# First mixer of a two-layer decode and prompt step: cached attention by halves of the heads, in four phases per group

## The chip, the cores and the metric

The program runs on one core of a Trainium2 chip. The core has five engines that work at once: TensorE (PE, matrix products; PEld are its weight loads), VectorE (DVE), ScalarE (ACT), GpSimd (POOL) and SyncE (SP, which here only issues transfers). Its 16 DMA engines bring data from HBM into the on-chip memory SBUF. The metric is the device time of the program in microseconds. The kernel before took 2915.26 us, the median of 3 runs (2914.95 to 2918.68).

## The reference, cut to what matters

The program does one step of a two-layer model for a prompt of 272 positions (16 of them meta tokens) and for 8 sequences that each bring 4 new tokens and have 2048 cached ones, in pages of 128. The change is in layer 0, in the attention of the 8 sequences over their cached pages. Each of the 8 heads has two score maps (m) over the same values, and the second is subtracted with a learned factor:

```python
def diff_attn_core(q, qpos, segs, lam):
    slopes = alibi_slopes(N_DH)
    qf = q.astype(jnp.float32) * (DK ** -0.5)
    scores = []
    for k, v, kpos in segs:
        s = jnp.einsum('bqhmd,bshmd->bhmqs', qf, k.astype(jnp.float32))
        dist = (qpos[:, None] - kpos[None, :]).astype(jnp.float32)
        s = s - slopes[None, :, None, None, None] * jnp.abs(dist)
        scores.append(jnp.where(dist >= 0, s, -jnp.inf))
    p = jax.nn.softmax(jnp.concatenate(scores, axis=-1), axis=-1)
    ...
    return out[:, :, :, 0] - lam * out[:, :, :, 1]

        k_past = cache_k[e, page_table].reshape(B, past_len, N_DH, 2, DK)
        v_past = cache_v[e, page_table].reshape(B, past_len, N_DH, DV)
        qpos = past_len + jnp.arange(T, dtype=jnp.int32)
        o = diff_attn_core(q, qpos, [(k_past, v_past, jnp.arange(past_len, dtype=jnp.int32)), (k, v, qpos)], lam)
```

Beside it in the same mixer stand the input projection (query, key, value, two convolution halves), the prompt's own attention, a causal depthwise convolution of width 31 with a layer norm, and the output projection. Everything is float32.

## The kernel before

All activations lie with their 2048 features over 16 tiles of 128 partitions and the 304 positions (272 of the prompt, 8 times 4 of the sequences) along the free dimension. A weight matrix is streamed as panels of 256 columns; a panel of the input projection is four *weight units* of 512 KB. ScalarE rounds a unit to a high part (`whi`, line 157), VectorE computes the rest (`wlo`, line 167), and TensorE makes three products for each of its eight tiles (lines 238 to 240), 24 in all.

Units and cache pages come through one ring of nine slots of 512 KB (`K.run`). SP issues all these transfers in program order, each as soon as its slots are free: line 118 a weight unit, line 1111 a key page, line 1194 a value page. A page's number is read from the page table in SBUF by SP itself just ahead of its transfer (`page`, lines 1099 to 1101), and the transfer's address is computed from it.

The decode attention works by two groups of four sequences. A *key unit* is two pages of keys of one sequence (two slots): eight products of 256 columns (line 1123), four heads beside each other in the four 32-column strips of TensorE's array. After the four sequences of a chunk, ScalarE copies the scores into `S` and VectorE takes the maxima (lines 1129, 1130). When all 16 pages are through, `k_new` (scores of the new tokens, maximum, four exponentials, line 1149), nine `transposes` (lines 1176 to 1185) and `k_norm` follow in one block. A *value unit* is one page (one slot): four products of 256 columns (line 1200). `v_copy` scales the sums of a sequence, `v_extract` picks out the diagonal pieces. New keys and values come from the projection of the same step (`k_done`, `v_done`).

The order is written out by `build`: `decode_jobs` lists the decode work, and `mix(i, W)` merges `SLOTS[i]` slots of it evenly with a stretch W of the weight panels. `tick` emits the pieces of the prompt's attention (`p_q` to `p_ln2`) and of the convolution (`tap`, line 1336) in between, by estimated time. The seven stretches are called stages 0 to 6 below; before, stage 0 holds six panels of keys and values and 62 slots, stage 1 the other two panels with a first one of the convolution, stages 3 and 4 the convolution's panels, stage 5 no weights, stage 6 the output projection's first half. The output projection's second half (`o_half`) needs all heads and ends the mixer.

Of the kernel before, what the change touches and what calls it, by code (L numbers as in the profile page):

```python
# [17 lines left out]
P = 128  # L18
T = 304
# [631 lines left out]
SLOTS = ((62,), (58,), (2,), (54,), (28,), (28,), (24,))  # L651
# [16 lines left out]
def const_l0():  # L668
# [4 lines left out]
    for e in range(2):  # L673
        for n in range(4):
            for u in range(4):
                c[:, C_E + e * 16 + n * 4 + u] = (q == n) & (j == 2 * (n % 2) + e) & (t == u)
# [6 lines left out]
    for hf in range(2):  # L683
        sl = np.array([SLOPES[4 * hf + a] for a in j])
        for g in range(2):
            for k in range(32):
                ok = (k // 4 == 4 * g + b4) & (k % 4 <= t)
                c[:, C_NB + g * 64 + hf * 32 + k] = np.where(ok, sl * (k % 4 - t), -BIG)
        for ch in range(8):
            base = 32 * (ch % 4) + 2 * hf  # L690
            o = C_BL + ch // 4 * P
            c[base, o:o + P] = sl
            c[base + 1, o:o + P] = sl * (256 * (ch - 7) - t)
            c[base, C_BR + 256 * hf:C_BR + 256 * hf + 256] = np.arange(256) - 256
            c[base + 1, C_BR + 256 * hf:C_BR + 256 * hf + 256] = 1.0
# [8 lines left out]
class L0(Sched):  # L704
# [4 lines left out]
    def __init__(self, k):  # L709
        self.k, self.nc = k, k.nc  # L710
        super().__init__(3)
        self.first, self.main, self.tail = self.queues
        self.low, self.debt = [], 0.0
        self.last = {}
        self.low_at = []
        self.gate = False
        self.st, self.al, self.pvs_, self.late = {}, {}, {}, []
        self.rvp = {}
        self.new_ready, self.waiting, self.pvs = False, [], {}


    def build(self):
# [25 lines left out]
        mix(0, kv[:30])  # L748
        mix(1, kv[30:] + cc[:4])
# [67 lines left out]
    def pan(self, name):  # L817
        return self.k.pp.tile([P, 512], F32, name=name, tag="side", bufs=2)


    def enter(self):
# [18 lines left out]
        self.mx = ap.tile([P, 2, 9], F32, name="mx")  # L840
        self.sc = ap.tile([P, 8], F32, name="scol")
# [116 lines left out]
    def p_v(self, h, j, st):  # L958
# [15 lines left out]
        nc.scalar.copy(self.vn[:, hc], pv[:32, 384:512])  # L974
        st["v"] = (vh, vl)
        st["vl"] = low

    def p_vl(self, st):
        for o, a, b in st.pop("vl"):
# [54 lines left out]
    def p_at(self, st, part):  # L1034
# [3 lines left out]
        pa = self.pan("pat")  # L1038
        if part == 0:
# [45 lines left out]
    def make_q(self):  # L1085


        nc = self.nc
        for g in range(2):
            for m in range(2):  # L1090
                r = slice(64 * m, 64 * m + 64)
                src = self.q[r, :, NP_ + 16 * g:NP_ + 16 * g + 16].rearrange("p h (b t) -> p h b t", b=4)
                a = self.qb[r, g]
                dst = bass.AP(tensor=a.tensor, offset=a.offset + 4 * m, ap=[a.ap[0], [P, 8], [40, 4], [1, 4]])
                nc.vector.tensor_copy(dst, src)
                d = self.qd[r, g].rearrange("p h (b m t) -> p h b m t", b=4, m=2)[:, :, :, m]
# [6 lines left out]
    def k_unit(self, b, c):  # L1103
# [4 lines left out]
        def load(raw):  # L1108
            for u in range(2):
                v = self.page(b, 2 * c + u)  # L1110
                nc.sync.dma_start(raw[:, u * 1024:(u + 1) * 1024],
                                  k.ins["ck"][bass.ds(v, 1)].rearrange("o p n -> p (o n)"))

        def use(raw):
            if b4 == 0:
                self.psS = k.pp.tile([P, 512], F32, name="psS", tag="cache", bufs=1)
                base, o = 32 * (c % 4), c // 4 * P
                nc.tensor.matmul(self.psS, self.bl[base:base + 4, o:o + P], self.bl[base:base + 4, 2 * P:],
                                 start=True, stop=False, tile_position=(base, 0))
            rv = raw.rearrange("p (u h s) -> p u h s", u=2, h=8)  # L1120
            for hf in range(2):
                for j in range(4):
                    nc.tensor.matmul(self.psS[32 * j:32 * j + 32, hf * 256:hf * 256 + 256],  # L1123
                                     self.qb[:, g, 4 * hf + j, 32 * b4:32 * b4 + 32], rv[:, :, 4 * hf + j],
                                     start=False, stop=(b4 == 3 and hf == 1), tile_position=(0, 32 * j))
            if b4 == 3:
                S = self.S[:, :, c * 256:c * 256 + 256]
                ps = self.psS.rearrange("p (h s) -> p h s", h=2)
                nc.scalar.copy(S, ps)
                nc.vector.tensor_reduce(self.mx[:, :, c], S, axis=AX.X, op=ALU.max)  # L1130
        return Job(use, load, 2 * UNIT, False, 2)

    def k_new(self, g):
        nc = self.nc
        ps = self.pan("psN")
        for h in range(8):
            hf, j = divmod(h, 4)
            nc.tensor.matmul(ps[32 * j:32 * j + 32, hf * 32:hf * 32 + 32], self.qd[:, g, h], self.kn[:, h],
                             start=(hf == 0), stop=(hf == 1), tile_position=(0, 32 * j))
        S = self.S[:, :, 2048:]  # L1140
        nb = self.cst[:, C_NB + 64 * g:C_NB + 64 * g + 64].rearrange("p (h s) -> p h s", h=2)
        nc.vector.tensor_tensor(S, ps[:, :64].rearrange("p (h s) -> p h s", h=2), nb, op=ALU.add)
        nc.vector.tensor_reduce(self.mx[:, :, 8], S, axis=AX.X, op=ALU.max)
        nm = self.sc[:, 0:2]
        nc.vector.tensor_reduce(nm, self.mx, axis=AX.X, op=ALU.max, negate=True)
        for z, cols in enumerate((slice(0, 1024), slice(1024, 2080))):
            for hf in range(2):
                s = self.S[:, hf, cols]
                nc.scalar.activation(s, s, AF.Exp, bias=nm[:, hf:hf + 1],
                                     accum_out=self.sc[:, 2 + 2 * z + hf:3 + 2 * z + hf])  # L1150

    def k_norm(self, g):

        nc = self.nc
        rv = self.sc[:, 6:8]
        nc.vector.tensor_tensor(rv, self.sc[:, 2:4], self.sc[:, 4:6], op=ALU.add)
        nc.vector.reciprocal(rv, rv)
        nc.vector.tensor_scalar(rv, rv, self.ls, None, op0=ALU.mult)
        rm = self.ap.tile([P, 2, 4], F32, name="rm")
        nc.vector.tensor_tensor(rm, self.cst[:, C_B4:C_B4 + 4].unsqueeze(1).to_broadcast([P, 2, 4]),  # L1160
                                rv.unsqueeze(2).to_broadcast([P, 2, 4]), op=ALU.mult)
        ps = self.pan("psr")
        for hf in range(2):
            nc.tensor.matmul(ps[64 * hf:64 * hf + 64, :4], self.cst[:, C_SEL:C_SEL + 64], rm[:, hf], start=True, stop=True,
                             tile_position=(0, 64 * hf))
        self.rvp[g] = self.ap.tile([P, 4], F32, name="rvp", bufs=2)
        nc.scalar.copy(self.rvp[g], ps[:, :4])

    def transposes(self, part):
# [3 lines left out]
        if part < 8:  # L1173
            for i in range(4):
                hf, pg = i // 2, 2 * part + i % 2
                nc.tensor.transpose(tr[:, i * P:i * P + P], self.S[:, hf, pg * P:pg * P + P], k.ident)
            for hf, copy in ((0, nc.scalar.copy), (1, nc.vector.tensor_copy)):
                src = tr[:, 256 * hf:256 * hf + 256].rearrange("p (g j b m) -> p g b j m", g=2, j=4, b=4)
                dst = self.S[:, hf, 256 * part:256 * part + 256].rearrange("p (g b j m) -> p g b j m", g=2, b=4, j=4)
                copy(dst, src)  # L1180
        else:
            for hf in range(2):
                nc.tensor.transpose(tr[:32, hf * P:hf * P + P], self.S[:, hf, 2048:], k.ident)
                src = tr[:32, hf * P:hf * P + P].rearrange("p (j b m) -> p b j m", j=4, b=4)
                nc.scalar.copy(self.PN[:, hf].rearrange("p b (j m) -> p b j m", j=4), src)

    def v_unit(self, b, pg):
# [4 lines left out]
        def load(raw):  # L1192
            v = self.page(b, pg)
            nc.sync.dma_start(raw, k.ins["cv"][bass.ds(v, 1)].rearrange("o p n -> p (o n)"))

        def use(raw):
            if pg == 0:
                self.pv = k.pp.tile([P, 512], F32, name="pvp", tag="cache", bufs=1)
            for n in range(4):
                nc.tensor.matmul(self.pv[32 * n:32 * n + 32, :256], self.S[:, n // 2, pg * P + 32 * b4:pg * P + 32 * b4 + 32],  # L1200
                                 raw[:, n * 256:n * 256 + 256], start=(pg == 0), stop=(pg == 15 and not self.new_ready), tile_position=(0, 32 * n))
            if pg == 15 and self.new_ready:
                self.new_values(self.pv, b4, False)
            if pg == 15:
                self.v_copy(b)
        return Job(use, load, UNIT, False)

    def new_values(self, ps, b4, start):
        for n in range(4):
            self.nc.tensor.matmul(ps[32 * n:32 * n + 32, :256], self.PN[:, n // 2, b4],  # L1210
                                  self.vn[:, n * 256:n * 256 + 256], start=start, stop=True, tile_position=(0, 32 * n))

    def v_copy(self, b):
        self.pvs[b] = self.ap.tile([P, 256], F32, name="pvs", bufs=4)
# [939 lines left out]
```

## Time and profile before

| | |
|---|---|
| runs, median (lowest to highest) | 2915.26 us (2914.95 to 2918.68) |
| profiled execution, its own time | 2920.92 us |
| its span, first to last instruction | 2919.2 us |
| TensorE, VectorE, ScalarE busy | 96%, 62%, 44% of the span |
| moved by DMA | 607.42 MB, mean 208 GB/s |
| mean granted TensorE clock | 0.977 of full |

The span is that of the one profiled execution. In a group, "x128" counts instructions, the busy time is that of the group together (overlaps counted once), and "idle before" with an arrow names what ended the wait. The trace counts two instructions for each matrix product of plain float32, so 64 key units of eight products stand as x1024. TensorE's products overlap, so the mean duration of one is longer than its share of the busy time.

### The profile page before, as it was taken

How to read it: one execution, taken by the hardware profiler on the slowest of the kernel's cores; microseconds unless marked ns; L12 is line 12 of the kernel's file. 1: busy time of each engine (PE TensorE's matmuls, PEld its weight loads, DVE VectorE, ACT ScalarE, POOL GpSimd, SP SyncE). 2: the span in 40 equal slices, each digit the busy share in tenths (PEclk: the TensorE clock that was granted, in tenths of full speed). 3: DMA queues.
4: the chain of work that ended last, by engine and by line, in shares of the span. 5: the costliest groups of instructions: out<-in, count | busy, mean ns of one | idle time of the engine just before them, and what ended most of it. 6: DMA issues, size and time to landing. Idle time of an engine off the chain costs nothing.

```text
span 2919.2 us, 56571 instructions
## 1 busy us (share of the span) xinstructions
PE 2794.5 (96%) x22621; PEld 2649.8 (91%) x22621; DVE 1801.1 (62%) x3153; ACT 1273.3 (44%) x2257; POOL 181.3 (6%) x417
## 2 busy tenths in 40 slices
PE   8998898698999999999999999899999999999997
PEld 8776676388999999999999999899899999999997
DVE  6454489735776677677676688655754454554555
ACT  4344222334534544544445567444534333333343
POOL 1011100001000111111110012000000000000000
PEclk9999999799999999999999999999999999999999
DMA  6887989794445656656665668565355555545553
GB/s 232 304 294 286 335 304 347 282 345 149 152 149 185 203 187 203 217 185 199 216 196 182 209 228 305 177 201 164 127 170 162 172 161 169 166 157 178 160 161 103
DMA packets 169914, 607.42 MB, mean 208 GB/s; under 512 B 20225, under 2 KB 22690, under 8 KB 169394
## 3 DMA queue, kind: packets, MB, share of 16 engines
q1 hardware_dynamic: 147522, 522.58, 54.0%
q0 software_dynamic: 20688, 76.24, 7.3%
q10 hardware_dynamic: 1440, 4.98, 0.5%
q8 instruction: 177, 2.90, 0.4%
q14 instruction: 87, 0.71, 0.1%
HBM read 563.63 MB, written 40.10 MB: 207 GB/s over the span
## 4 chain that ended last, share of the span: by engine, by line
PE 73%; DVE 5%; issue 5%; DMA 2%; ACT 2%; POOL 1%; SPq 0%; DVEq 0%; POOLq 0%; ACTq 0%
PE pan L238 23%; PE pan L239 23%; PE pan L240 23%; DMA ring<-in_w_cc 1%; PE pvp L1200 1%; DVE wlo L167 1%; DMA scr<-scra 1%; DVE oc L1336 1%; DVE odd L1336 1%; PE stp L1785 0%; ACT whi L157 0%; PE yps L2013 0%; POOL scr L1900 0%; DMA ring<-in_cv 0%; PE skp L1793 0%
## 5 line engine op out<-in xcount | busy, mean ns | idle before, releaser
L167 DVE TENSOR_TENSOR wlo<-ring,whi 128x1024 fp32r<-128x1024 f32 (+1 forms) x738 | 884.1, 1201 | 677.7 <-ACT whi L157 674.2
L157 ACT CAST whi<-ring 128x1024 fp32r<-128x1024 f32 (+1 forms) x738 | 758.7, 1029 | 1121.4 <-PE pan L239 922.6
L238 PE MATMUL pan<-hh,whi 128*128 128x304 f32 (+1 forms) x3936 | 1204.7, 306 | 23.4 <-ACT hh L506 16.5
L240 PE MATMUL pan<-hh,wlo 128*128 128x304 f32 (+1 forms) x3936 | 1188.7, 302 | 11.7 <-DVE wlo L167 11.7
L239 PE MATMUL pan<-hl,whi 128*128 128x304 f32 (+1 forms) x3936 | 1188.0, 302 | 1.8 <-DVE hl L509 1.5
L238 PEld LDWEIGHTS pan<-hh,whi 128*128 128x128 f32 x3936 | 749.5, 190 | 56.9 <-issue 24.0
L240 PEld LDWEIGHTS pan<-hh,wlo 128*128 128x128 f32 x3936 | 749.3, 190 | 15.6 <-DVE wlo L167 15.6
L239 PEld LDWEIGHTS pan<-hl,whi 128*128 128x128 f32 x3936 | 749.6, 190 | 4.7 <-DVE hl L509 4.5
L238 PE MATMUL pan<-mh,whi 128*128 128x304 f32 (+1 forms) x1408 | 422.1, 300 | 0.0
L240 PE MATMUL pan<-mh,wlo 128*128 128x304 f32 (+1 forms) x1408 | 419.8, 298 | 0.0
L239 PE MATMUL pan<-ml,whi 128*128 128x304 f32 (+1 forms) x1408 | 419.7, 298 | 0.0
L238 PEld LDWEIGHTS pan<-mh,whi 128*128 128x128 f32 x1408 | 265.0, 188 | 1.0 <-issue 1.0
L240 PEld LDWEIGHTS pan<-mh,wlo 128*128 128x128 f32 x1408 | 265.1, 188 | 0.0
L239 PEld LDWEIGHTS pan<-ml,whi 128*128 128x128 f32 x1408 | 264.9, 188 | 0.0
L1200 PE MATMUL pvp<-ring,xs 128*32 128x256 f32 x1024 | 78.1, 432 | 12.6 <-DMA ring<-in_cv 7.4
L579 DVE TENSOR_TENSOR u<-g,u 128x304 f32<-128x304 f32 (+1 forms) x88 | 41.1, 467 | 69.1 <-ACT g L578 67.2
L393 DVE TENSOR_TENSOR sqa<-sqa,sqt 128x304 f32<-128x304 f32 (+1 forms) x78 | 36.6, 469 | 58.9 <-ACT sqt L389 57.8
L386 POOL MEMSET sqt<- 128x80 f32 x4 | 0.7, 165 | 1131.7 <-DVE sqa L393 1131.7
L577 DVE TENSOR_TENSOR u<-pan,rs 128x304 f32<-128x304 f32 (+1 forms) x88 | 40.8, 464 | 46.1 <-PE pan L240 46.1
L1200 PEld LDWEIGHTS pvp<-ring,xs 128*32 128x32 f32 x1024 | 29.8, 120 | 43.5 <-issue 13.8
L581 DVE TENSOR_TENSOR ml<-u,mh 128x304 fp32r<-128x304 f32 (+1 forms) x88 | 41.1, 467 | 44.5 <-ACT mh L580 44.5
L1123 PE MATMUL psS<-ring,qb 128*32 128x256 f32 x1024 | 67.0, 387 | 0.0
(371 smaller groups left out, 2885.2 us busy)
## 6 DMA issues: line engine op xcount, KB each, us to landing
ring<-in_w_gu SPq DMA_DIRECT2D x352, 512.0 KB, 3.6
ring<-in_ck SPq DMA_DIRECT2D x128, 512.0 KB, 5.7
ring<-in_cv SPq DMA_DIRECT2D x128, 512.0 KB, 6.0
ring<-in_w_dn SPq DMA_DIRECT2D x128, 512.0 KB, 3.7
ring<-in_w_qkv SPq DMA_DIRECT2D x48, 512.0 KB, 7.1
ring<-in_w_dn SPq DMA_DIRECT2D x64, 384.0 KB, 3.1
ring<-in_w_cc SPq DMA_DIRECT2D x32, 512.0 KB, 6.7
ring<-in_w_oe SPq DMA_DIRECT2D x32, 512.0 KB, 6.5
```

The lines of the kernel that those rows point to most:

```text
L157: nc.scalar.copy(j.hi[:, :n], j.raw[:, :n])
L167: nc.vector.tensor_tensor(j.lo[:, :n], j.raw[:, :n], j.hi[:, :n].bitcast(F32), op=ALU.subtract)
L238: mm(out, wh, xh, start=start, stop=False)
L239: mm(out, wh, xl, start=False, stop=False)
L240: mm(out, wl, xh, start=False, stop=stop)
L393: nc.vector.tensor_tensor(self.sq[:, c0:T], self.sq[:, c0:T], t[:, c0:T], op=ALU.add)
L577: nc.vector.tensor_tensor(u, pu, rs, op=ALU.mult)
L579: nc.vector.tensor_tensor(u, g, u, op=ALU.mult)
L581: nc.vector.tensor_tensor(self.ml[:, m, c0:], u, self.mh[:, m, c0:].bitcast(F32), op=ALU.subtract)
L1123: nc.tensor.matmul(self.psS[32 * j:32 * j + 32, hf * 256:hf * 256 + 256], self.qb[:, g, 4 * hf + j, 32 * b4:32 * b4 + 32], rv[:, :, 4 * hf ...
L1200: nc.tensor.matmul(self.pv[32 * n:32 * n + 32, :256], self.S[:, n // 2, pg * P + 32 * b4:pg * P + 32 * b4 + 32], raw[:, n * 256:n * 256 + ...
L1336: nc.vector.scalar_tensor_tensor(c, src, w, c, op0=ALU.mult, op1=ALU.add)
```

## The change

The head halves (heads 0 to 3, heads 4 to 7) are taken apart. The caches are laid out with the half as an outer index, a transfer brings half a page (128 partitions by 512 elements), and `half_page` reads the page number for each. A key unit is four half pages of one sequence (two slots), a value unit two half pages of consecutive pages (one slot). Each group has four phases: keys of half 0, keys of half 1, values of half 0, values of half 1; the softmax steps of a half stand between the units of the phase after it. Three query panels come ahead of the decode work instead of four, the fourth goes into stage 0 with all eight key and value panels, and `SLOTS` changes. `hold` has two subtractions of the prompt's attention emitted before their bank is taken again.

```diff
-SLOTS = ((62,), (58,), (2,), (54,), (28,), (28,), (24,))
+SLOTS = ((56,), (56,), (2,), (48,), (28,), (28,), (34,))
...
-        js, off = k.panels("w_qkv", 0, 4, ks, *hs, (0, T), self.q_done, start)
+
+        js, off = k.panels("w_qkv", 0, 3, ks, *hs, (0, T), self.q_done, start)
         k.jobs += js
-        k.call(self.make_q)
+        k.call(self.make_q, 0)
+        q4, off = k.panels("w_qkv", off, 1, ks, *hs, (0, T), lambda p, a, b: self.q_done(3, a, b))
+        q4.append(Job(lambda: self.make_q(1)))
...
-        mix(0, kv[:30])
-        mix(1, kv[30:] + cc[:4])
+        mix(0, q4 + kv)
+        mix(1, cc[:4])
         mix(2, [])
...
+    def half_page(self, raw, name, b, pg, hf):
+        v = self.page(b, pg)
+        self.nc.sync.dma_start(raw, self.k.ins[name][bass.ds(v, 1), hf].rearrange("o p n -> p (o n)"))
+
+    def k_unit(self, b, hf, c):
...
-            for u in range(2):
-                v = self.page(b, 2 * c + u)
-                nc.sync.dma_start(raw[:, u * 1024:(u + 1) * 1024],
-                                  k.ins["ck"][bass.ds(v, 1)].rearrange("o p n -> p (o n)"))
+            for u in range(4):
+                self.half_page(raw[:, u * 512:u * 512 + 512], "ck", b, 4 * c + u, hf)
...
+            rv = raw.rearrange("p (u h s) -> p u h s", u=4, h=4)
+            for j in range(4):
+                nc.tensor.matmul(self.psS[32 * j:32 * j + 32], self.qb[:, g, 4 * hf + j, 32 * b4:32 * b4 + 32], rv[:, :, j],
+                                 start=False, stop=(b4 == 3), tile_position=(0, 32 * j))
             if b4 == 3:
...
+    def k_exp(self, hf, z):
+        s = self.S[:, hf, (slice(0, 1024), slice(1024, 2080))[z]]
+        self.nc.scalar.activation(s, s, AF.Exp, bias=self.sc[:, hf, 0:1], accum_out=self.sc[:, hf, 1 + z:2 + z])
...
+    def v_unit(self, b, hf, pp):
...
+            for u in range(2):
+                self.half_page(raw[:, u * 512:u * 512 + 512], "cv", b, 2 * pp + u, hf)
...
+            for u in range(2):
+                for n in range(2):
+                    r = 64 * u + 32 * n
+                    o = (2 * pp + u) * P + 32 * b4
+                    nc.tensor.matmul(self.pv[r:r + 32, :256], self.S[:, hf, o:o + 32], raw[:, u * 512 + n * 256:u * 512 + n * 256 + 256],
+                                     start=(pp == 0), stop=(pp == 7 and not (new and u == 0)), tile_position=(0, r))
...
+        def keys(g, hf):
+            nonlocal todo
+            phase([[self.k_unit(4 * g + b, hf, c)] for c in range(4) for b in range(4)], (1, 2, 3, 5, 6, 7, 8, 9, 10))
+            todo = [step(self.k_new, g, hf), step(self.k_exp, hf, 0), step(self.k_exp, hf, 1)]
+            todo += [step(self.transposes, hf, i) for i in range(5)] + [step(self.k_norm, g, hf)]
+
+        def values(g, hf):
+            units = []
+            for b in range(4 * g, 4 * g + 4):
+                for pp in range(8):
+                    units.append([self.v_unit(b, hf, pp)])
...
+            phase(units, (2, 4, 6, 9, 11, 13, 15, 17, 19))
         for g in range(2):
...
+            keys(g, 0)
+            keys(g, 1)
+            values(g, 0)
+            values(g, 1)
+            J.append(step(self.v_extract, 4 * g + 3, 1))
         return J
...
-    o["ck"] = np.ascontiguousarray(ck.reshape(n, P, 8, 128).transpose(0, 3, 2, 1)).reshape(n, P, 1024)
-    o["cv"] = np.ascontiguousarray(np.asarray(inp["cache_v"])[0].reshape(n, P, 1024))
+    o["ck"] = np.ascontiguousarray(ck.reshape(n, P, 2, 4, 128).transpose(0, 2, 4, 3, 1)).reshape(n, 2, P, 512)
+    o["cv"] = np.ascontiguousarray(np.asarray(inp["cache_v"])[0].reshape(n, P, 2, 512).transpose(0, 2, 1, 3))
```

What this does to SP's order is seen in stage 6, where a weight unit of the output projection (`w_oe`) is followed by value pages (`cv`). Before, a slot of values there is these rows behind the weight unit:

```order
L118 DMA ring<-in_w_oe 128x1024
L1101 TENSOR_LOAD pt
L1101 ISA x2
L1194 ISA
L1194 DMA ring<-in_cv 128x1024
```

After, it is these (line 1115 reads the page number, line 1119 issues the half page):

```order
L118 DMA ring<-in_w_oe 128x1024
L1115 TENSOR_LOAD pt
L1115 ISA x2
L1119 ISA
L1119 DMA ring<-in_cv 128x512
L1115 TENSOR_LOAD pt
L1115 ISA x2
L1119 ISA
L1119 DMA ring<-in_cv 128x512
```

The number load, the register work and the transfer stand twice for the same slot, with half the elements each.

On TensorE the softmax of group 0 moves. Before, in stage 1, the last products of a weight unit (`pan`) are followed by all transposes of both halves (`tr`), the normalising product (`psr`) and then the first value products (`pvp`):

```order
L240 MATMUL pan<-hh,wlo_94 128x304
L1176 MATMUL tr<-ident,xs 128x128 x32
L1183 MATMUL tr<-ident,xs 32x128 x2
L1164 MATMUL psr<-rm,cst 64x4 x2
L1200 MATMUL pvp<-ring_90,xs 32x256 x4
```

After, in stage 1 too, the transposes of half 1 stand between the value units of half 0 (line 1213; `pvp<-vn` are the new values, `ex` the extraction of a sequence):

```order
L1213 MATMUL pvp<-ring,xs 32x256 x8
L1258 MATMUL ex<-cst,pvs 128x2x4 x2
L1186 MATMUL tr<-ident,xs 128x128 x4
L1213 MATMUL pvp<-ring,xs 32x256 x4
L1213 MATMUL pvp<-ring_90,xs 32x256 x4
L1186 MATMUL tr<-ident,xs 128x128 x4
L1213 MATMUL pvp<-ring_90,xs 32x256 x4
L1213 MATMUL pvp<-ring,xs 32x256 x4
```

One block of 32 transposes has become groups of four with two value units between them, and no weight product stands in this piece.

## Rows read from the trace of the kernel before

**Rows 1.** The page: engine totals, then busy tenths in 40 slices of 73 us.
```profile
PE 2794.5 (96%) x22621; PEld 2649.8 (91%) x22621; DVE 1801.1 (62%) x3153; ACT 1273.3 (44%) x2257; POOL 181.3 (6%) x417
...
PE   8998898698999999999999999899999999999997
...
DMA  6887989794445656656665668565355555545553
```

**Rows 2.** Table by stretch: us of PE, PEld, DVE, ACT, POOL; clock, DMA share, GB/s.
```profile
73.40:231.00 157.60, 149.85 (x1313) 119.96 (x1313) 77.77 (x217) 60.34 (x146) 16.20 (x55) 0.99 0.84 301
231.00:337.00 106.00, 94.55 (x837) 68.99 (x837) 46.65 (x149) 41.88 (x113) 14.55 (x60) 0.94 0.81 298
349.00:530.00 181.00, 158.58 (x1324) 122.19 (x1316) 152.81 (x308) 44.64 (x68) 0.00 (x0) 0.92 0.82 301
530.00:576.00 46.00, 32.82 (x317) 17.69 (x317) 35.92 (x91) 10.35 (x22) 1.78 (x4) 0.78 1.00 362
...
775.00:800.00 25.00, 25.00 (x181) 25.00 (x181) 18.59 (x37) 11.04 (x15) 0.00 (x0) 1.00 0.51 167
700.00:2919.00 2219.00, 2170.28 (x17400) 2151.74 (x17398) 1384.92 (x2198) 1026.89 (x1765) 136.27 (x265) 0.99 0.56 180
```

**Rows 3.** Instructions of two lines on SP: ns minimum/median/maximum, first and last start.
```profile
L1101 SPq TENSOR_LOAD <-pt x256: 262/268/1239, 34.5 to 630.7; - x128
...
L1194 SPq DMA_DIRECT2D ring<-in_cv x128: 332/333/537, 218.3 to 633.2; - x128
...
DMA to landing us min/median/max: 3.4/6.0/12.6
```

**Rows 4.** Timeline of SP: start us, us from first issue to last, line, operation, count.
```profile
41.67 10.29 SPq L1111 DMA_DIRECT2D ring<-in_ck  x4
...
337.15 0.38 SPq L118 DMA_DIRECT2D ring<-in_w_cc  x1
...
376.06 1.43 SPq L1111 DMA_DIRECT2D ring<-in_ck  x2
...
379.13 3.77 SPq L1111 DMA_DIRECT2D ring<-in_ck  x4
...
529.47 0.34 SPq L118 DMA_DIRECT2D ring<-in_w_cc  x1
...
576.26 0.38 SPq L118 DMA_DIRECT2D ring<-in_w_oe  x1
...
586.86 1.49 SPq L1194 DMA_DIRECT2D ring<-in_cv  x2
...
633.24 0.33 SPq L1194 DMA_DIRECT2D ring<-in_cv  x1
```

**Rows 5.** Waits of SP from 73 to 231 us: total, times, longest.
```profile
SPq L1111 <- PE psS L1123: 60.2, 19, 5.6
```

**Rows 6.** TensorE's groups up to 680 us (busy, mean ns), and the bias product's line.
```profile
L1200 PE MATMUL pvp<-ring,xs 128*32 128x256 f32 x1024 | 78.1, 432 | 12.6 <-DMA ring<-in_cv 7.4 <-ACT pvs L1215 5.3
L1123 PE MATMUL psS<-ring,qb 128*32 128x256 f32 x1024 | 67.0, 387 | 0.0
L1176 PE MATMUL tr<-ident,xs 128*128 128x128 f32 x64 | 14.6, 392 | 12.9 <-ACT xs L1149 6.9 <-DVE xs L1180 5.5
...
L1118 PE MATMUL psS<-bl x16: 489/494/500, 73.4 to 493.4; 4*128 4x512 f32 x16
```

**Rows 7.** Timeline of the second softmax: start us, us, idle before in brackets.
```profile
514.28 0.69 PE L1176 MATMUL tr<-ident,xs 128*128 128x128 f32 x2 [5.73 <-ACT xs L1149]
...
524.80 0.28 PE L1183 MATMUL tr<-ident,xs 128*32 128x128 f32 x1 [0.34 <-ACT PN L1185]
```

**Rows 8.** Instructions of the convolution's tap line.
```profile
L1336 DVE SCALAR_TENSOR_TENSOR oc<-cx,small,oc x120: 492/497/510, 360.5 to 556.6; 128x272 f32<-128x272 f32 x120
```

**Rows 9.** Chain of waits at the end of the first mixer: start us, us.
```profile
657.64 0.36 PE ex L1238 x4
...
663.07 0.62 PE pan L238
```

More of the change, by code (lines that the diff above doesn't have):

```diff
@@ L718, in __init__ @@
         self.rvp = {}
-        self.new_ready, self.waiting, self.pvs = False, [], {}
+        self.vn_done, self.waiting, self.pvs = set(), [], {}
+        self.npan, self.holds = 0, []
     def build(self):
@@ L817, in pan, with hold @@
     def pan(self, name):
+        self.npan += 1
+        while self.holds and self.holds[0][0] <= self.npan - 2:
+            self.holds.pop(0)[1]()
         return self.k.pp.tile([P, 512], F32, name=name, tag="side", bufs=2)
+    def hold(self, fn):
+        self.holds.append((self.npan, fn))
     def enter(self):
@@ L1143, in k_new @@
[L1143 to L1150, printed above, removed]
@@ L1152, in k_norm @@
-    def k_norm(self, g):
+        for j in range(4):
+            h = 4 * hf + j
+            nc.tensor.matmul(ps[32 * j:32 * j + 32, :32], self.qd[:, g, h], self.kn[:, h], start=True, stop=True,
+                             tile_position=(0, 32 * j))
+        S = self.S[:, hf, 2048:]
+        o = C_NB + 64 * g + 32 * hf
+        nc.vector.tensor_tensor(S, ps[:, :32], self.cst[:, o:o + 32], op=ALU.add)
+        nc.vector.tensor_reduce(self.mx[:, hf, 4:5], S, axis=AX.X, op=ALU.max)
+        nm = self.sc[:, hf, 0:1]
@@ L1162, in k_norm @@
         ps = self.pan("psr")
[L1163 to L1169, printed above, removed]
+        for z in range(2):
+            nc.tensor.matmul(ps[64 * z:64 * z + 64, :4], self.cst[:, C_SEL:C_SEL + 64], rm, start=True, stop=True,
+                             tile_position=(0, 64 * z))
@@ L1171, in transposes @@
+        self.rvp[g, hf] = self.ap.tile([P, 4], F32, name="rvp", bufs=3)
+        nc.scalar.copy(self.rvp[g, hf], ps[:, :4])
+    def transposes(self, hf, part):
         nc, k = self.nc, self.k
         tr = self.pan("tr")
-        if part < 8:
+        if part < 4:
             for i in range(4):
[L1175 to L1180, printed above, removed]
-        else:
[L1182 to L1185, printed above, removed]
@@ L1192, in load @@
         def load(raw):
[L1193 to L1194 removed]
+            for u in range(2):
+                self.half_page(raw[:, u * 512:u * 512 + 512], "cv", b, 2 * pp + u, hf)
         def use(raw):
[L1197 removed]
+            if pp == 0:
                 self.pv = k.pp.tile([P, 512], F32, name="pvp", tag="cache", bufs=1)
[L1199 to L1201 removed]
@@ L1202, in use @@
[L1202 to L1205, printed above, removed]
-        return Job(use, load, UNIT, False)
[L1208 to L1214, printed above, removed]
-        self.nc.scalar.activation(self.pvs[b], self.pv[:, :256], AF.Copy, scale=self.rvp[b // 4][:, b % 4:b % 4 + 1])
-        if not self.new_ready:
-            self.waiting.append(b)
+            new = pp == 7 and self.ready(hf)
@@ new lines, in v_unit, with ready, new_values, v_copy @@
+        return Job(use, load, UNIT, False)
+    def ready(self, hf):
+        return all(h in self.vn_done for h in range(4 * hf, 4 * hf + 4))
+    def new_values(self, ps, b4, hf, start):
+        for n in range(2):
+            o = (2 * hf + n) * 256
+            self.nc.tensor.matmul(ps[32 * n:32 * n + 32, :256], self.PN[:, hf, b4], self.vn[:, o:o + 256], start=start,
+                                  stop=True, tile_position=(0, 32 * n))
+    def v_copy(self, b, hf, new):
+        self.pvs[b, hf] = self.ap.tile([P, 256], F32, name="pvs", bufs=4)
+        self.nc.scalar.activation(self.pvs[b, hf], self.pv[:, :256], AF.Copy, scale=self.rvp[b // 4, hf][:, b % 4:b % 4 + 1])
+        if not new:
+            self.waiting.append((b, hf))
+            assert len(self.waiting) <= 4
```

143 lines of the change are left out of this document (70 added, 73 removed).

## The prediction

> **What bounds the kernel now.** I read the page first, to see where time can be won or lost at all. Over the whole span TensorE is 96% busy; its row in tenths is weak only in the first nine slices, the first mixer, where the DMA row stands at 7 to 9 [rows 1]. From 700 us on the change touches nothing, and TensorE is busy 2170 of 2219 us there [rows 2]. So the question is the first mixer alone, which ends when its output projection starts, at 663 us.
>
> The table by stretch comes next. I cut it where the decode work and the weights change their mix (the entries of SLOTS, called stages 0 to 6 here): the keys of group 0 up to 231 us, its values up to 337, the gate panels with the keys of group 1 up to 530, a stretch without weights up to 576, and the rest. The reader is to see that DMA moves about 300 GB/s in the first three and 362 GB/s at a full share in the fourth, while TensorE is busy about 90% of the first three [rows 2]. One fetched 512 KB (a ring slot) costs 0.524 MB / 362 GB/s = 1.45 us of DMA time at that rate.
>
> Then the queue that issues those transfers, SyncE's (SP). It is never shown as busy on the page, but its own rows show what a cache page costs there: a load of the page number (0.27 us) and the issue (0.33 us) [rows 3], with register work and gaps between. Where nothing holds it, four pages go out in 3.77 us and two in 1.49 us [rows 4]: a pitch of (3.77 - 0.33)/3 = 1.15 and 1.49 - 0.33 = 1.16 us; another pair takes 1.43, so 1.10. I take 1.12 us a page. A weight unit takes 0.38 us and a gap, 0.47. In the old kernel a page is a whole slot, so 1.12 is under the 1.45 us that DMA wants: SP has slack, and from 73 to 231 us it waits 60 us in 19 waits for a free slot behind the key products [rows 5].
>
> **What the change does to each part.** *The issue.* A page becomes two half pages, each with its own page number load and its own DMA; the two pieces of SP's order show it. The number of cached DMAs goes from 256 to 512 and a slot costs SP 2 x 1.12 = 2.24 us instead of 1.12. The same 0.524 MB every 2.24 us is 234 GB/s, less than each stretch from 73 to 576 us moves today [rows 2]. SP therefore becomes the bound wherever TensorE needs less than 2.24 us per slot with what stands beside it. A half page may take longer per byte on the DMA engines, which no row shows; down to 234 GB/s that hides behind SP, so I cost it at nothing.
>
> *TensorE's products.* 64 key units cost 67.0/64 = 1.05 us each now, in 16 instructions; then 8 instructions of twice the width. Same columns: 1.05 us; at the same time per instruction 0.52 us. I take 1.05, as the width doubles. Value pages cost 78.1/128 = 0.61 us with waits, unchanged [rows 6].
>
> *The softmax.* Now the transposes stand in a block: the first waits 5.73 us for the exponential, from 508.5 us, and the last ends at 525.1 with copies between [rows 7]. That is 16.5 us in which no page is used, taken twice 33 us. Afterwards each step stands between units of the next phase (the two pieces of TensorE's order) and that stall goes. What is late next there is the page itself, so the 33 us return only where SP isn't the bound. Doubled small steps (8 more copies on ScalarE, which is busy 45 of 181 us there [rows 2], and 8 more extractions) lie in SP's time too.
>
> *The hold list and make_q.* The low halves of the attention are issued before their bank is taken again: the same subtractions, earlier, in the half of VectorE's time that is free in stage 0 (78 of 158 us busy [rows 2]); nothing, or their own length where the next weight's low half stands behind one, under 0.5 us each. make_q(0) is 8 copies of half the width ahead of the first key unit, as many as now at full width: nothing.
>
> *The earlier start.* Key units begin one panel of four weight units sooner. A weight unit is 24 products of 25.00/181 = 0.138 us, 3.31 us [rows 2], so the first key unit moves from 73.4 [rows 6] to about 73.4 - 13.2 = 60 us.
>
> **The sum, by stages.** Instruction counts are from the program's order.
> Stage 0 (36 weight units, 28 key units, 56 slots) is TensorE's. Before, from 73.4 to 231 us, 157.6 us held 25 weight units (83), 32 key units (34), 8 bias products of 0.49 [rows 6] (4), so 37 us for 78 of the 144 score products with all that follows them and its waits. 108 of 144 come in the new stage 0: 52 us. Then 119 + 29 + 3 + 52 and 17 transposes of 14.6/64 = 0.23 [rows 6] (4) make 207 us, and the stage ends at 267. SP needs 56 x 2.24 + 36 x 0.47 = 142 us, so it waits.
> Stages 1 and 2 (58 slots, 4 weight units) are SP's. It can be 8 slots ahead, the ring has nine: 50 x 2.24 + 2 = 114 us, to 381. TensorE needs about 13 + 31 + 17 + 10 = 71 us of these. Before, the first transfer of stage 3 left at 337.15 [rows 4]: 44 us later.
> Stages 3 and 4 (76 slots, 28 weight units): 170 + 13 = 183 us. VectorE has its taps here, 153 us busy of 181 before [rows 2], in instructions of 0.50 us that also hold back the low halves of the weights [rows 8]; I add 10 us for pages waiting on them, to 574. Before, SP was there at 529.8: 44 us later.
> Stage 5 (28 slots, no weights): 63 us, to 637, against 576.26 [rows 4]: 61 us later.
> Stage 6 and what is left (38 slots, 16 weight units): 85 + 8 = 93 us, to 730, against 633.6 for the last page [rows 4]: 97 us later.
> The tail gets shorter, because nothing is queued up any more when the last page lands: landing 3.4 us at least [rows 3], its products 0.6, and 657.6 to 663.1 for extraction and normalising [rows 9], with 3 us for copies between: 12 us against 29.5. The projection starts at 742 instead of 663, 79 us later, and all after it keeps its length. On the profiled execution's own 2920.9 us that is 3000; the median of the runs is 5.7 us below that one, so 2995 us.
>
> *Both ends.* Pitch 1.10 or 1.16 over the 192 slots behind stage 0: -8 or +15. Stage 0 with the key units at 0.52 us: -15; without the 7.8 us that TensorE was idle in its stretch [rows 2]: -10; with as much again: +10. The taps: none (-10) or 30 us (+20). The clock: where TensorE waited for pages the granted clock was 0.78 [rows 2], between the two levels of 1.2 and 2.4 GHz, and at 1.2 the 71 us of stage 1 would be 142, 28 more than SP's 114: +28 at most. Not all come together: 2950 to 3045.
>
> **Rules weighed.** The page number load takes 0.27 us in 256 cases [rows 3]. The Trainium skill (DMA: Bandwidth & Descriptors, Latency and other measured facts) gives about 600 ns as the floor of a tensor load; by that the pitch would be 1.45 us and the 192 slots 127 us longer, an estimate of 3122 us from that page. The trace disagrees, and I keep 1.12.
>
> The rows show SP spending 1.12 us to start a transfer that DMA needs 1.45 us for [rows 2, 4]. The Trainium skill (the same page, Issuing engines are not separate DMA queues) says that the time to initiate a DMA is usually small relative to the DMA itself. By it halving the pages would be free, which is the first rival below; the rows speak against it.
>
> **Rivals.** First, *the issue hides and the stalls go: faster.* If the second half of a page cost SP less than 1.45 - 1.12 = 0.33 us more, transfers would still set the pace, and the two softmax blocks would be won: 2915 - 33 = 2882 us. It decides at a pitch of 0.73 us. For it: SP waits for slots now. Against it: no burst in the trace runs under 1.10, and the new order repeats the same rows. Chance 5%.
> Second, *SP is the bound but never waits: no change.* 512 x 1.12 + 83 x 0.47 = 612 us from about 28 us (41.67 [rows 4] less the panel), last page at 640, and with the short tail 652 instead of 663; with some waits, 663. 2904 to 2921. It needs SP to run ahead through stage 0, and nine slots allow 20 us of that. Chance 3%.
> Third, *worse, through clock and taps:* the two upper ends together, 2995 + 28 + 20 + 15 = 3058 us and more. For it: VectorE is 84% busy where pages come late. Against it: SP's wait leaves both engines room. Chance 10%.
>
> **How the numbers follow.** The forecast has 82%: 2995 us. The range, 2950 to 3045, leaves out the first two rivals and most of the third, and a little of the forecast's own low end. Under 0.2%, some 6 us, this kernel's measurement tells nothing apart. Faster takes the first rival and the faster half of the second, 6%; same 2%; slower the rest, 92%.
>
> **What would show it.** Right: SP's pages about 1.12 us apart for long stretches without waits, 512 of them; DMA at about 234 GB/s from some 270 us on; TensorE's value products waiting for the cache pages; the longest loss without weights (stage 5) and in stages 1 and 2; the span after the projection starts unchanged. Wrong: pairs of half pages under 1.5 us apart, DMA back over 300 GB/s behind stage 0, or a first mixer that ends before 700 us. If stage 0 ends far from 267 us, its attention pieces were mis-sized.

## The result and the profile after

The changed kernel takes 3011.89 us (median; 3010.89 to 3019.32), against 2916.97 (2914.95 to 2929.19) for the kernel before (its three runs above and a fourth): a ratio of 1.032, 95% interval 1.029 to 1.036. It is slower, by some 95 us. The profiled execution took 3010.89 us, its span 3009.0. The forecast was 2995, its range 2950 to 3045.

The page first, the rows that answer to [rows 1] (totals of the engines, TensorE's tenths and the GB/s by slice of 75 us):

```profile
PE 2834.4 (94%) x22149; PEld 2647.9 (88%) x22149; DVE 1803.4 (60%) x3180; ACT 1275.2 (42%) x2267; POOL 183.0 (6%) x417
...
PE   8998788768899999999999999899899999999997
...
GB/s 249 282 250 225 233 301 291 253 250 305 162 155 150 196 195 202 212 182 207 206 202 180 189 212 293 240 161 198 136 168 158 170 164 168 168 164 168 168 160 102
```

From the twelfth slice on the two kernels' rows for TensorE read alike. Ahead of it TensorE has lost a tenth or more in the fifth, sixth, ninth and eleventh slices, and DMA moves 225 and 233 GB/s in the fourth and fifth. Next the table by stretch (columns as in [rows 2]), cut at 267 us, where stage 0 was forecast to end, and behind it at times of SP's timeline below (376, 577, 639 and 738 us):

```profile
60.00:267.00 207.00, 204.01 (x1449) 161.99 (x1441) 112.72 (x311) 85.06 (x207) 27.55 (x84) 0.99 0.79 253
267.00:376.00 109.00, 79.63 (x602) 45.42 (x602) 22.97 (x86) 20.55 (x59) 7.92 (x39) 0.84 0.79 233
376.00:577.00 201.00, 163.72 (x1115) 117.90 (x1113) 157.85 (x317) 42.87 (x62) 2.07 (x8) 0.92 0.88 285
577.00:639.00 62.00, 39.10 (x273) 13.89 (x271) 39.63 (x105) 22.26 (x51) 1.77 (x4) 0.78 0.83 237
639.00:738.00 99.00, 79.81 (x656) 63.54 (x655) 19.79 (x24) 22.46 (x37) 0.00 (x0) 0.90 0.87 283
```

Up to 267 us TensorE is busy 204 of 207 us. Behind that neither TensorE (73%, 81%, 63%, 81%) nor DMA (233 to 285 GB/s, where 362 was reached before) is full. What is full is SyncE's queue, which the page never shows as busy. Its instructions, to be read against [rows 3] (ns minimum/median/maximum):

```profile
L1115 SPq TENSOR_LOAD <-pt x512: 262/268/1236, 23.9 to 737.4; - x171
L1115 SPq FUSED_REGOPS  x512: 152/152/178, 24.5 to 737.7; - x171
L1115 SPq SEQ_ASSERT  x512: 18/18/28, 24.7 to 737.9; - x171
...
L1119 SPq FUSED_REGOPS  x512: 42/50/56, 24.8 to 738.0; - x171
...
L1119 SPq DMA_DIRECT2D ring<-in_cv x256: 337/338/671, 257.3 to 738.2; - x128
```

SP's timeline, against [rows 4], with the end of stage 0's weights and with the runs of half pages that no weight unit interrupts:

```profile
24.98 3.78 SPq L1119 DMA_DIRECT2D ring<-in_ck  x4
...
232.83 0.34 SPq L118 DMA_DIRECT2D ring<-in_w_qkv  x1
233.22 0.42 SPq L118 DMA_DIRECT2D ring<-in_w_cc  x1
...
339.45 37.03 SPq L1119 DMA_DIRECT2D ring<-in_cv  x32
376.58 0.38 SPq L118 DMA_DIRECT2D ring<-in_w_cc  x1
...
577.39 61.83 SPq L1119 DMA_DIRECT2D ring<-in_cv  x52
639.32 0.38 SPq L118 DMA_DIRECT2D ring<-in_w_oe  x1
...
737.02 1.49 SPq L1119 DMA_DIRECT2D ring<-in_cv  x2
```

A run of 52 half pages takes 61.83 us: a pitch of (61.83 - 0.34)/51 = 1.21 us; the run of 32 gives 1.18. SP's largest wait from 267 to 760 us (total, times, longest; against [rows 5]) shows that it is hardly waiting for slots:

```profile
SPq L1119 <- PE pvp L1213: 9.4, 33, 0.4
```

It is 9.4 us, in 33 waits of 0.4 us at most. TensorE in turn waits for half pages, up to 760 us for 28.8 us in 38 waits, where its value products waited 7.4 us for pages before [rows 6]:

```profile
PE pvp L1213 <- DMA ring<-in_cv: 28.8, 38, 4.1
PE pvp L1213 <- ACT pvs L1233: 27.9, 9, 7.4
PE psr L1175 <- DVE rm L1172: 12.0, 3, 6.4
```

The other two rows, for ScalarE's copy of a sequence's values and for the normalising product's input, come back in the experiments. The end of the first mixer in the chain of waits answers to [rows 9]:

```profile
743.61 0.57 PE pvp L1213 x8
744.18 0.34 PE pan L238
747.73 0.57 PE pvp L1213 x8
748.29 0.57 PE pvp L1228 x4
...
755.35 0.62 PE pan L238
```

The output projection starts at 755.35 us instead of 663.07, 92.3 us later; the execution is 90.0 us longer (3010.89 against 2920.92). The whole loss lies ahead of that point.

### The profile page after: what moved, and what is told of

It reads as the page before. It is cut to its first block, busy times and chain, and to the rows that moved or that the text cites. A ratio compares the mean times of both kernels' runs of the same rounds, so it can differ in the third digit from the quotient of the medians.

```text
span 3009.0 us, 57453 instructions
## 1 busy us (share of the span) xinstructions
PE 2834.4 (94%) x22149; PEld 2647.9 (88%) x22149; DVE 1803.4 (60%) x3180; ACT 1275.2 (42%) x2267; POOL 183.0 (6%) x417
## 4 chain that ended last, share of the span: by engine, by line
PE 81%; DVE 6%; DMA 5%; ACT 3%; issue 2%; SPq 2%; POOL 0%; DVEq 0%; ACTq 0%; POOLq 0%
PE pan L238 25%; PE pan L240 25%; PE pan L239 24%; DMA ring<-in_cv 2%; PE pvp L1213 1%; DVE wlo L167 1%; DMA ring<-in_w_cc 1%; SPq L1115 1%; SPq L1119 1%; ACT whi L157 1%; PE psS L1138 1%; DMA ring<-in_w_oe 1%; PE yps L2047 1%; PE sps L1979 1%; PE stp L1819 0%
## 5 line engine op out<-in xcount | busy, mean ns | idle before, releaser
L1213 PE MATMUL pvp<-ring,xs 128*32 128x256 f32 x1024 | 102.0, 429 | 57.8 <-DMA ring<-in_cv 28.8
L1138 PE MATMUL psS<-ring,qb 128*32 128x512 f32 x512 | 70.1, 626 | 4.4 <-DVE qb L1109 3.0
```

Source lines behind the costliest of these rows:

```text
L1138: nc.tensor.matmul(self.psS[32 * j:32 * j + 32], self.qb[:, g, 4 * hf + j, 32 * b4:32 * b4 + 32], rv[:, :, j], start=False, stop=(b4 == 3) ...
L1213: nc.tensor.matmul(self.pv[r:r + 32, :256], self.S[:, hf, o:o + 32], raw[:, u * 512 + n * 256:u * 512 + n * 256 + 256], start=(pp == 0), s ...
```

## The experiments

Theory: SP's time to read a page number and issue a half page sets the pace behind stage 0. Rival A: half pages are slow on the DMA engines. Rival B: the new order (phases, softmax between units) is what costs. Each ratio is to the kernel before, with its 95% interval.

**Half pages in the old order.** The caches' layout of the changed kernel, and in both units:

```diff
-            v = self.page(b, pg)
-            nc.sync.dma_start(raw, k.ins["cv"][bass.ds(v, 1)]...)
+            for hf in range(2):
+                v = self.page(b, pg)
+                nc.sync.dma_start(raw[:, hf * 512:hf * 512 + 512], k.ins["cv"][bass.ds(v, 1), hf]...)
```

> The order of the kernel before, but each page fetched as two half pages, each with its own page number load. Theory (SP's issue time): a slot costs SP 2.4 us (two times the 1.2 us seen between value half pages of the changed kernel), so the same stretches become SP's and it is 70 to 110 us slower than before, 2987 to 3027 us. Rival A (half pages of 2 KB rows are slow to move on the DMA engines): as slow, 2990 to 3030. Rival B (the new order of phases costs the time): 2917, no change. Tells B from the other two.

Measured: 3020.81 us, 1.033 (1.031 to 1.035). The doubled issue in the old order brings a loss as large, so B falls as its cause; A still stands here. With half pages the two orders can't be told apart: their intervals overlap.

**The changed kernel with fixed page numbers.** The page table isn't read; page i stands for the i-th entry, so other pages are fetched, as many and as large.

```diff
-        return self.nc.sync.value_load(self.pt[0:1, i:i + 1], min_val=0, max_val=159)
+        return i
```

> The changed kernel with fixed page numbers: the page table isn't read, so the pages are others than the reference's. Transfers, rows, order and products are the same, SP only issues (0.34 us a half page and a gap, about 0.9 us a slot). Theory: SP is no bound any more, the softmax blocks stay hidden: 2870 to 2920 us, and value stretches move over 350 GB/s. Rival A: DMA stays at about 235 GB/s and the time at 3000 to 3012. Rival B: over 2980.

Measured: 2925.19 us, 1.0015 (1.0004 to 1.0026), above the 2870 to 2920 of the theory. Two pieces of SP's timeline and the stretch of this run in which DMA is fullest:

```profile
293.83 17.85 SPq L1119 DMA_DIRECT2D ring<-in_cv  x28
...
369.28 1.75 SPq L1119 DMA_DIRECT2D ring<-in_cv  x4
```

```profile
577.00:639.00 62.00, 60.85 (x570) 48.93 (x563) 16.36 (x22) 19.58 (x31) 0.00 (x0) 1.00 1.00 371
```

Half pages leave 0.65 us apart in the long run, and DMA moves 371 GB/s of them and weights: A falls. In that run SP waits for slots again (9.3 us in 23 waits). In the burst of four they leave (1.75 - 0.33)/3 = 0.47 us apart, so an issue without a number takes 0.47 us or less, where one with a number takes 1.15 in a burst. But the gain of the order that the theory also expected did not come.

**The kernel before with fixed page numbers,** the same edit as a control.

> Control: the kernel before with fixed page numbers (the page table isn't read, so the pages are others than the reference's), whole pages. Theory: SP had slack with 1.12 us a page against 1.45 us of transfer, so no change: 2908 to 2922 us. If reading the number had bound the old kernel somewhere too, 2890 to 2905, and the gain of the fixed numbers in the changed kernel would be partly this.

Measured: 2914.03 us, 0.998 (0.997 to 0.999), within the 2908 to 2922, though the 0.2% are clear of noise; whether they come from the numbers or from the other pages, no run tells. So with SP out of the way the new order is 11 us slower than the old one, by intervals that don't meet. TensorE's waits from 231 to 665 us, first in this run, then in the changed kernel with fixed numbers:

```profile
PE pan L240 <- DVE wlo L167: 9.1, 11, 2.4
...
PE pan L238 <- ACT whi L157: 6.0, 5, 4.1
PE tr L1176 <- DVE xs L1180: 6.0, 3, 4.0
PE tr L1176 <- ACT xs L1149: 5.2, 2, 4.5
PE pvp L1200 <- ACT pvs L1215: 5.0, 4, 3.1
```

```profile
PE psr L1175 <- DVE rm L1172: 15.0, 3, 8.2
PE pvp L1213 <- ACT pvs L1233: 12.1, 9, 4.4
PE psS L1134 <- ACT xs L1142: 7.1, 4, 4.5
...
PE pan L238 <- ACT whi L157: 4.1, 2, 2.3
...
PE pan L240 <- DVE wlo L167: 2.2, 3, 1.0
```

The old block made TensorE wait 6.0 + 5.2 us for the softmax. The new order waits 15.0 us for the normalising product's input (`rm`), 12.1 instead of 5.0 for ScalarE to copy a sequence's values out of their bank, and 7.1 for it to copy scores out of theirs. Against that it waits 6.3 us for its weights' two parts (4.1 + 2.2) and the old order 15.1 (6.0 + 9.1), so the longer waits of one kind are in part paid back by the other. Of the changed kernel's 27.9 us for the values' bank, these 12.1 are left when SP is freed; its 12.0 for `rm` don't shrink.

**A number read twice in the kernel before,** whole pages and one transfer each:

```diff
+        self.nc.sync.value_load(self.pt[0:1, i:i + 1], min_val=0, max_val=159)
         return self.nc.sync.value_load(self.pt[0:1, i:i + 1], min_val=0, max_val=159)
```

> The kernel before with each page number read twice, one transfer of the whole page as before. Prices the reading alone: a page costs SP 1.15 + 0.27 + 0.3 (register work and gaps) = 1.7 us, above the 1.45 us of its transfer only where value pages come without weights. Theory: 5 to 30 us slower, 2922 to 2947 us. If the loss comes from the second transfer and not from SP's time: 2917.

Measured: 2940.25 us, 1.0076 (1.006 to 1.009), as expected. SP's timeline in it:

```profile
252.28 7.18 SPq L1195 DMA_DIRECT2D ring<-in_cv  x5
```

Five pages in 7.18 us: (7.18 - 0.33)/4 = 1.71 us each, now over the 1.45 of the transfer, and 0.5 to 0.6 us over a single load's 1.12 to 1.2: reading and checking a number costs that much of SP's time.

**One load for the numbers of a unit,** four for keys, two for values, in the changed kernel:

```diff
+        _, vs = self.nc.values_load_multi_w_load_instructions(self.pt[0:1, i:i + n], engines=[mybir.EngineType.SP],
+                                                              min_val=0, max_val=159)
+        for u, v in enumerate(vs):
+            self.nc.sync.dma_start(raw[:, u * 512:u * 512 + 512], ...)
```

> The changed kernel with the page numbers of a unit (four of a key unit, two of a value unit) read by one load. Theory: a key half page costs 0.27/4 + 0.17 + 0.34 + 0.15 = 0.73 us of SP's time, a value half page 0.27/2 + 0.66 = 0.80: a slot 1.46 to 1.6 us, about what its transfer takes. 2885 to 2930 us. Rivals A and B: 3000 to 3015.

Measured: 2986.1 us, 1.022 (1.019 to 1.024): a miss. SP's instructions in it (the check's register work, the loads in a stretch of key units, the loads in one of value units):

```profile
L1119 SPq FUSED_REGOPS  x512: 147/152/181, 24.6 to 713.6; - x171
...
L1119 SPq TENSOR_LOAD <-pt x10: 296/301/304, 430.6 to 467.7; - x10
...
L1119 SPq TENSOR_LOAD <-pt x16: 468/472/487, 340.0 to 374.0; - x16
```

A load of four numbers takes 301 ns and one of two 472 (medians), where one number takes 268: four at once save 0.19 us each, two at once 0.03. The register work of the range check stays, 512 times. So little was won for the values: 52 half pages of them still take 60.05 us, 1.17 each. Why two numbers take longer than four stays open.

**The same without the range check** (in the multiple load, `skip_runtime_bounds_check_because=...`).

> The changed kernel with one load for all page numbers of a unit and no range check of them on SP. Reading several numbers at once brought SP's pitch only from 1.18 to 1.10 us, since the register work and check of each number stayed. Theory: without these a value half page costs about 0.8 us and a key half page 0.7, a slot 1.4 to 1.6: near the fixed numbers' 2925, 2922 to 2945 us. If other things than SP's time hold the changed kernel: 2975 to 2990.

Measured: 2930.82 us, 1.004 (1.002 to 1.005), as expected. `FUSED_REGOPS` of 152 ns and `SEQ_ASSERT` are gone from SP, and 52 half pages leave in 47.07 us:

```profile
531.19 47.07 SPq L1123 DMA_DIRECT2D ring<-in_cv  x52
```

That is 0.92 us each. The check, 0.17 us of instructions a number, gave back 55 us (2986.1 to 2930.82).

**Every second half page issued by GpSimd,** changed kernel, number and transfer:

```diff
+        eng = self.nc.gpsimd if pg % 2 else self.nc.sync
+        v = eng.value_load(self.pt[0:1, i:i + 1], min_val=0, max_val=159)
+        eng.dma_start(raw, ...)
```

> The changed kernel with every second half page issued by GpSimd, with its own number load there. Theory: a slot costs each queue 1.2 us if GpSimd needs no longer than SP; then 2880 to 2930 us; if GpSimd's issue takes 2 us or its other work waits behind slots, up to 2970. Rival A and B: 3000 to 3015.

Measured: 2940.77 us, 1.006 (1.004 to 1.008), above the 2880 to 2930 expected if GpSimd is as quick as SP. A second issuing queue takes back 71 of the 95 us, with as many half pages in the same order, as the theory has it and the rivals don't. GpSimd was nearly as quick: where nothing holds it, its half pages leave some 1.24 us apart.

**The wait for the normalising product eased,** on top of the load without check: VectorE's part of `k_norm` goes out with the third transposes.

```diff
-            todo += [step(self.transposes, hf, i) for i in range(5)] + [step(self.k_norm, g, hf)]
+            todo += [step(self.transposes, hf, i) for i in range(2)]
+            todo += [Job(lambda: (self.k_rows(g, hf), self.transposes(hf, 2)))]
+            todo += [step(self.transposes, hf, i) for i in range(3, 5)] + [step(self.k_norm, g, hf)]
```

> As multi_skip, with VectorE's part of the normalising (four small operations) issued three steps before its product on TensorE. With fixed numbers the product waited 15.0 us in 3 waits for it. Theory: with SP out of the way such waits are what the new order has left over; 8 to 15 us under multi_skip, 2912 to 2935 us, at best level with the kernel before. If the waits only move to the next thing: within 4 us of multi_skip.

Measured: 2925.88 us, 1.002 (1.001 to 1.003), 5 us under the load without check: less than the 8 to 15 expected, but each of its 12 runs is under the lowest of those 4. TensorE's wait for the product shrinks from 15.0 to 4.0 us (231 to 665 us), the one for the values' bank grows from 17.1 to 19.6. This wait was real, but part of the 11 us only.

**Slots moved between the stages** of that kernel, first out of stage 6, then into it:

```diff
-SLOTS = ((56,), (56,), (2,), (48,), (28,), (28,), (34,))
+SLOTS = ((56,), (56,), (2,), (50,), (28,), (36,), (24,))
```

> skip_split (0.2% above the kernel before) with ten slots moved out of the last attention stage: stages 3, 5 and 6 take 50, 36 and 24 slots where they took 48, 28 and 34. Theory: the cheap-issue versions of the new order lose at the end, where 38 slots in a row are bound by transfers at about 369 GB/s (2.1 us a slot), while the DMA engines have room in stage 5. Then ten slots fewer at the end take 10 x 2.1 = 21 us off it and up to ten are put back on stages 3 and 5 where work of TensorE (0.5 to 1 us a slot) is added: 2908 to 2920 us, a ratio of 0.996 to 1.000. The rival, that the new order loses in its waits for the softmax of the half (PE behind ACT and DVE), expects that moving slots does nothing or less than 3 us: 2923 to 2930.

```diff
+SLOTS = ((56,), (56,), (2,), (48,), (28,), (20,), (42,))
```

> skip_split with eight slots moved the other way, out of stage 5 into stage 6 (20 and 42 slots where they were 28 and 34). Moving eight slots into stage 5 and two into stage 3 cost 21 us (skip_slots), so stage 6 has cover that those stages lack. Theory: a slot costs about 2.7 us in stage 5, where the transfer of the mixer's work leaves it on the path, and 0.5 us or less in stage 6: eight moved slots gain 8 x 1.5 to 2.2 us, 2908 to 2916 us, a ratio of 0.996 to 1.000. The rival, that stage 6 with DMA at 367 GB/s has no room left and 28 and 34 is already the balance, expects each moved slot to cost 2 us or so: 2926 to 2945.

Measured: 2946.77 us, 1.010 (1.008 to 1.011), and 2935.17 us, 1.0055 (1.004 to 1.007): both moves cost, and both expectations of a gain fell. SP's first weight unit of stage 6 and its last pages in the kernel with 34 slots there, with 24, and with 42:

```profile
572.40 0.37 SPq L118 DMA_DIRECT2D ring<-in_w_oe  x1
...
646.70 0.87 SPq L1123 DMA_DIRECT2D ring<-in_cv  x2
```

```profile
599.79 0.37 SPq L118 DMA_DIRECT2D ring<-in_w_oe  x1
...
668.74 1.70 SPq L1123 DMA_DIRECT2D ring<-in_cv  x2
```

```profile
558.34 0.37 SPq L118 DMA_DIRECT2D ring<-in_w_oe  x1
...
657.04 0.92 SPq L1123 DMA_DIRECT2D ring<-in_cv  x2
```

Stage 6 lasts 74.3, 68.9 and 98.7 us. Ten slots fewer save 5.4 us there, while the stages ahead take 27.4 us longer; eight more cost 24.4, 3.1 us a slot, and save 14.1 ahead. Of these three tables that of the change is the best.

**The kernel before without the range check,** and **with six slots moved from stage 5 to 6** (22 and 30):

> The kernel before, whole pages, its order, with the one number of a page loaded without the range check. If the check is what made the several-number load expensive (theory: the loss is SyncE's time per number), it is also in the kernel before and shows where SyncE runs without a pause: fixed numbers took 3 us off that kernel, so 2910 to 2917 us, a ratio of 0.997 to 1.000. The rival, that the check costs nothing by itself and only several loads at once gained by its loss, expects 1.000 to 1.001.

> The kernel before, whole pages and its order, with six slots moved from stage 5 to stage 6 (22 and 30 where they were 28 and 24). If slots are cheaper in stage 6 in the old order too: 2906 to 2914 us, a ratio of 0.996 to 0.999. If 28 and 24 is already the balance there (DMA at 343 GB/s in stage 6): 2918 to 2930, a ratio of 1.001 to 1.005.

Measured: 2918.99 us, 0.9997 (0.9987 to 1.0008), and 2919.52 us, 0.9998 (0.9987 to 1.0008): no difference, and the second meets neither of its ranges. In the old kernel an issue with its number takes SP less time than the page's transfer (1.15 against 1.45 us), and dropping the check buys nothing that can be measured. No version that keeps reading the table beat the kernel before.

## Why the prediction was right

The bound and its place were forecast rightly. That the time came out within 17 us of 2995 is in part luck: two sizes were wrong in opposite directions, stage 0 by 15 us and SP's time behind it by 23.

*The bound.* SP behind stage 0, from three sides: the doubled issue alone loses 101 us (to 2919.49 in its own comparison), taking the numbers away returns 87, a second queue 71.

*Stage 0.* Forecast 207 us of TensorE from 60, to 267. It began at 59.5, and by the count of TensorE's products its 36th and last weight unit was done at some 252 us, 15 us sooner; by the timeline above SP had gone on to stage 1's weights (`w_cc`) at 233. Up to 267 SP waits mostly behind key products, 53 us in all, as forecast:

```profile
SPq L118 <- PE psS L1138: 30.9, 15, 5.6
SPq L1119 <- PE psS L1138: 22.3, 9, 8.6
```

Mis-sized was the term of the attention pieces, 52 us for 108 score products, worked out from 37 us for 78. The old trace has 90 in that stretch, 30 on each of three lines, of which this is the first; the new stage 0 has the 108, 36 a line:

```profile
L238 PE MATMUL psc<-kh,qp x30: 274/283/390, 98.6 to 226.9; 128*128 128x256 f32 x20, 128*16 128x272 f32 x10
```

```profile
L238 PE MATMUL psc<-kh,qp x36: 274/282/390, 100.0 to 249.1; 128*128 128x256 f32 x24, 128*16 128x272 f32 x12
```

By 90 they come to 44 us instead of 52, half of the 15; the rest fits the waits that the 37 us held (TensorE was idle 7.8 us there [rows 2], but 1.7 us of the new stage 0). The key units took 70.1/64 = 1.10 us against 1.05:

```profile
L1138 PE MATMUL psS<-ring,qb 128*32 128x512 f32 x512 | 70.1, 626 | 4.4 <-DVE qb L1109 3.0
```

*The pitch.* Forecast 1.12 us with an end of 1.16; measured 1.18 and 1.21 over the long runs, outside that end. Most steps there are 1.16 to 1.17 us. In the run of 52, five of the 51 steps are longer, 1.48 to 2.14 us, and add 2.6 us; three of them hold a load of a number that took 0.70 to 1.24 us instead of 0.27. [rows 4] had 1.15 and 1.16 beside one 1.10, and the sum took a value between.

*The stages on SP* (forecast, measured): end of 2 at 381, 376.6; of 4 at 574, 572; of 5 at 637, 639.3; last page at 730, 738.2. (By `SLOTS` the last key unit, the four half pages from 571.8 us on, already belongs to stage 5.) Stage by stage SP took longer than forecast: 125 us instead of 114 for stages 1 and 2, 195 instead of 193 for 3 and 4, 67.5 instead of 63 for stage 5, 99 instead of 93 from there to the last page, 23 us in all. The pitch alone comes to 0.06 to 0.09 x 2 x 192 = 23 to 35; in stages 3 and 4 the 10 us allowed for the taps took most of it up. That only 8 show at the last page comes from the 15 us by which stage 0 ended early.

*The tail.* Forecast 12 us, measured 755.35 - 738.2 = 17.2. The step that failed is "nothing is queued up any more": from the last page to the end of its products it took 10 us (748.29 - 738.2) instead of 4.0, because products of the output weights (line 238) still stood between the value products at 734 to 748 us. From there on it was 7.1 us, where 8.4 were allowed.

*The sum.* Start of the projection +92.3 against +79: 8 from the pages (23 of SP less the 15 of stage 0) and 5 from the tail. What follows came out 2.3 us shorter, so 3010.9 against 3000 for the profiled execution. The other 6 us of the miss in the median is the offset of the old profiled execution (5.7 us above its median), which the new one doesn't have (1.0 us below).

*A sign.* DMA was to move about 234 GB/s from some 270 us on. It does where half pages go all but alone (233 and 237 GB/s). With weights between them it moves 285 and 283, and two slices of the page show 301 and 305, over the 300 that the prediction named as a sign of being wrong: it had counted the pages alone, and a weight unit brings twice a half page's bytes for an issue of 0.38 us.

*The rule weighed.* A half page at 371 GB/s is 0.262 MB / 371 = 0.71 us of transfer, and SP needs 1.16 to 1.21 us to start it. The Trainium skill (DMA: Bandwidth & Descriptors, Issuing engines are not separate DMA queues) holds that issuing on several engines saves only the time to initiate, usually small relative to the DMA; here that time is the larger one, and the second issuing engine was worth 71 us.

*The rivals.* The first was priced at 2882 us from a pitch of 0.73 on. The fixed numbers met its condition, with 0.65 us between half pages, and gave 2925. Its price was wrong: of the 33 us that I took for the stall of two softmax blocks, TensorE waited 12.4 (6.9 + 5.5, which stood in [rows 6]); most of the rest was work that remains (the 64 transposes alone 14.6 us). And where the old order with fixed numbers waits 16.2 us in the three rows on softmax and copies shown above (6.0 + 5.2 + 5.0), the new one waits 34.2 (15.0 + 12.1 + 7.1). So this rival fell on its price too, not only on its condition. The second didn't occur, since SP was done 98 us after the time that it asks for (738 against 640), nor did the third: 3012 us stays under its 3058, with the granted clock at 0.84 from 267 to 376 us.

Open stays why the new order with fixed numbers is 11 us slower: eased, the wait of 15.0 us gave 5 us in another version of it; slots moved in either direction cost more, so the rest was not found.

## What to carry to other kernels

Halving a transfer whose address is read at run time doubles a serial cost that the page doesn't show as busy: before splitting, compare the issuing queue's pitch for one transfer (here 1.2 us, of it 0.5 to 0.6 for reading and checking the number) with the time of the transfer that is left (0.71). Where the queue must carry it, first drop the range check or split the issue between two engines, which gave back 55 us (with the numbers of a unit in one load) and 71 us here, then ask what is gained. And price a stall by the waits of the engine that stands still, not by the length of the block in which they stand: 12 us of 33 were waits.

## What the runs showed that was not expected

Reading two page numbers with one load hardly helps, reading four does: 472 ns for a load of two, 301 for a load of four, 268 for one number. The range check behind it, 152 + 18 ns of instructions on SP for each of 512 numbers (87 us in sum), was worth 55 us of the kernel's time where SP was the bound, and nothing measurable in the kernel before (0.9987 to 1.0008).
